# A fast matrix multiplication in a ConvGLU up-projection: the third panel combined in ten of eleven groups, and the order of its weight sums

## The chip, the cores and the metric

The kernel runs on one core of a Trainium2 chip. The core has a matrix engine (TensorE, PE in the profile; its weight loads are PEld), a vector engine (VectorE, DVE), a scalar engine (ScalarE, ACT), a general engine (GpSimd, POOL) and a queue that issues most transfers (SyncE, SP). Each engine works through its own instructions in order and waits on semaphores for the others. Matmuls write into PSUM banks; all else lives in SBUF. The metric is the device time of one execution in microseconds (us); shown is the median of several.

## The reference

One layer of a streaming encoder for two groups of requests: 256 frames of a new stream and 8 x 16 frames of running streams, 384 rows in all. The first half (a convolution branch, an attention branch, gates, an output projection) is not touched by the change. The second half is a ConvGLU feed-forward:

```python
h2 = rmsnorm(x, norm_ffn_g)
up = h2 @ w_up                      # 2048 -> 2 x 5632
g_half = up[..., :D_FF]
u_half = up[..., D_FF:]
ext_f = jnp.concatenate([ffn_buf.astype(g_half.dtype), g_half], axis=1)
gc = causal_dwconv(ext_f, ffn_dw_w, ffn_dw_b)      # 3 taps
x = x + (jax.nn.silu(gc) * u_half) @ w_down
```

All of it is float32.

## The kernel before

**Precision.** Every float32 operand X of a matmul is split into a rounded half `hi` and a remainder `lo = X - hi`, and a product is three matmuls: hi by hi, hi by lo, lo by hi. For a block of weights (2 x 128 rows of 512 columns, 512 KB) the split is a copy on ScalarE (L167, `hi`) and a subtraction on VectorE (L168, `lo`). `ahead` keeps `depth[0]` blocks split in advance: two, and three in the feed-forward part, where a third pair of halves is there. The halves of item i go into the pair that item i-3 has left. The raw blocks come through SyncE (L150) into slots, three at first and seven in the feed-forward part, used in turn.

**The up-projection.** It runs in eleven groups of 512 gate columns and the 512 up columns that belong to them (`up_group`, g = 0 to 10). The 2048 inputs are four panels q of 512. The order of the whole is a list: up 0, up 1, up 2, down (0, 1), up 3, up 4, down (2, 3), and so on to up 9, up 10, down (8, 9, 10). Between two "down" stages there are thus two up groups (three at first).

**Plain and combined panels.** In a plain panel each of the two halves of the rows is an item of its own for the up side (`pu0`, `pu1`) and the gate side (`pg0`, `pg1`): four blocks, four items, 6 products of 3 matmuls each, 24 products in all. In a combined panel the four blocks B11, B12, B21 and B22 are used as in Winograd's form of a fast 2 x 2 multiplication: there are seven items, b22, t3, t1, b11, t2, b21 and t4, of 4, 4, 2, 4, 2, 4 and 2 products, 22 in all. Four of the items are sums of weights, made by VectorE on whole blocks: t3 = B22 + B12 (L209, into one of three sum tiles), t1 = B12 + B11 (L214, in place), t2 = t3 + B11 and t4 = t2 + B21 (L218, in place in the sum tile). Each of the seven is then split like any block. So a combined panel has three splits and four sums more than a plain one, and 6 matmuls less.

Panels 0 and 1 are combined in all groups ("double"); panel 2 (`BOTH`) also in the groups in `TRIPLE`, 3, 5, 7 and 9 ("triple"). A double group has 92 products, 276 matmuls; a triple one 90 products, 270 matmuls. Of panel 2 both kinds of input halves are kept; the combinations of its rows (`xm`) are made by `combined` during the output projection before, a number of ticks (9 matmuls each there) after the panel's output.

**The order within a group** is given by `steps(g)`. The upper pass takes for each combined panel b22, t3, t1, then a plain up item if there is one left to spread, then b11, t2; then come the remaining plain up items; the lower pass starts with `pg0` of the first plain panel and goes on with b21 and t4 of each combined panel. In group 0 no plain item is put into the upper pass. TensorE follows this order as written. VectorE, ScalarE, GpSimd and SyncE are ordered by a scheduler ahead of the run, by what it thinks is ready and by rank: splits and sums are issued with a rank 150 instructions ahead of their place, the evacuations of banks with 250. A sum may so be placed anywhere ahead of the split that needs it.

**Banks and evacuation.** Products add up in five banks `acc` and three `misc`. `q6` (L1225 to L1230) is four operations on VectorE and one on ScalarE, done after the last t2 of the upper pass; it frees the bank of P5, which Q4 takes in the lower pass. `p7` (L1219) and `p1` (L1222) are copies on ScalarE, `q3`, `q2`, `p2`, `q4` (L1234, L1237, L1251, L1254) one operation on VectorE each.

**After a group** come its taps: from the eighth tick of three products on, four times in turn a fill of the extended rows on ScalarE and GpSimd, three taps (L1142 on ScalarE, L1144 twice on VectorE), a SiLU, the product with the up half and its split. They run beside the stage that follows: for groups 0, 1, 3, 5, 7 and 9 that is another up group, for groups 2, 4, 6 and 8 a down stage.

Of the kernel before, what the change touches and what calls it, by code (L numbers as in the profile page):

```python
# [11 lines left out]
ALU = mybir.AluOpType  # L12
# [20 lines left out]
KEYS_FIRST, KEYS_EVERY = 40, 14  # L33
SPLIT_AHEAD, EVAC_AHEAD, FFN_AHEAD = 150, 60, 250
BOTH = 2
TRIPLE = (3, 5, 7, 9)
SPARE = 1


# [9 lines left out]
def hybrid_step(  # L49
# [41 lines left out]
    def f(ap):  # L91
        return ap.bitcast(F32)
# [3 lines left out]
    tt = nc.vector.tensor_tensor  # L96
# [7 lines left out]

    newest = {}

    def queued(d, chain=True):
        e = d.ins.engine
        if chain and e in newest:
            tc.add_manual_dep(d.ins, newest[e], mybir.DependencyInfo(  # L110
                mybir.DependencyClass.NoSync, mybir.DependencyReason.DATA), reason="queue")
        newest[e] = d.ins.name

    def load_x(c, n, sample_queue=None):
# [43 lines left out]
    def split(raw, o, by_row=False):  # L158
        n = splits[0] % depth[0] - 2
        splits[0] += 1  # L160
        if n >= 0:
            hi, lo = pairs_more[n]
        else:
            hi = wp.tile([P, 2, 512], F32R, tag="hi", bufs=2, name="hi")
            lo = wp.tile([P, 2, 512], F32R, tag="lo", bufs=2, name="lo")
        for k in (slice(0, 1), slice(1, 2)) if by_row else (slice(0, 2),):
            nc.scalar.copy(hi[:, k, :o], raw[:, k, :o])  # L167
            tt(lo[:, k, :o], raw[:, k, :o], f(hi[:, k, :o]), op=ALU.subtract)  # L168
        return hi, lo

    plan = []
# [9 lines left out]
    sums, new_sum = {}, []  # L181

    def steps(g):
        mixed = mixed_of(g)
        pu, pg = ([(f"p{side}{h}", q) for q in range(4) if q not in mixed for h in range(2)] for side in "ug")
        n = len(pu) // 2 if g else 0
        top, low = [], pg[:1]
        for i, q in enumerate(mixed):
            top += [(what, q) for what in ("b22", "t3", "t1")] + pu[i:min(i + 1, n)]
            top += [(what, q) for what in ("b11", "t2")]  # L190
            low += [("b21", q), ("t4", q)] + (pg[i + 1:i + 2] if len(mixed) == 2 else [])
        return top + pu[n:] + low + pg[len(mixed) + 1 if len(mixed) == 2 else 1:]

    def planned_mixed(w, c1, c2, g):
        held = {}

        def load(rows):
            return fetch([rows])[0]
# [4 lines left out]
        def single(name, k, c):  # L203
            held[name] = load(rows_of(w, k, c, 512))
            return held[name]

        def both(q):
            sums[q] = new_sum[0](q)
            tt(sums[q], held["b22"][:], single("b12", 4 * q, c2)[:], op=ALU.add)  # L209
            return sums[q]  # L210

        def across(q):
            b = held["b12"][:]
            tt(b, b, single("b11", 4 * q, c1)[:], op=ALU.add)  # L214
            return b

        def grown(q, name):
            tt(sums[q], sums[q], held[name][:], op=ALU.add)  # L218
            return sums[q]

        make = {"b22": lambda q: single("b22", 4 * q + 2, c2), "t3": both, "t1": across,
# [2 lines left out]
        for what, q in steps(g):  # L224
            if what[0] == "p":
                k, c = 4 * q + 2 * int(what[2]), {"u": c2, "g": c1}[what[1]]
# [38 lines left out]
    def after(units, fn):  # L265
        later.append([units, fn])
# [391 lines left out]
    z, e, r, s2, pl = tiny("lz"), tiny("le"), tiny("lr"), tiny("ls"), tiny("lpoly")  # L658
# [98 lines left out]
    def load_v(h):  # L757
# [14 lines left out]
                  k=kv[h // 4][:, :, :, h % 4, :]) for h in range(H)]  # L772
# [100 lines left out]
    for h in range(H):  # L873
        v = heads[h]["q"]
        hi, lo = (natural(aHL[h // 4][:, i, h % 4, :]) for i in range(2))
# [134 lines left out]
    def combined(n, d):  # L1010
# [22 lines left out]
        def plain():  # L1033
            hi, lo = xm[n]
            for j, (t, h) in enumerate(((0, 0), (0, 1), (1, 1), (2, 0), (2, 1))):
                nc.scalar.copy(blocks(hi[:, 5 + j]), of(t, h))
                tt(blocks(lo[:, 5 + j]), of(t, h), blocks(f(hi[:, 5 + j])), op=ALU.subtract)
        later_by = 5 if n == BOTH else 0
        after(5 + later_by, add_up)
        after(6 + later_by, halves)  # L1040
        if n not in xg:
            after(7, plain)

# [306 lines left out]
```

## Time and profile before

| | |
|---|---|
| Median of 3 runs (lowest, highest) | 1977.36 us (1973.34, 1980.31) |
| Profiled execution, its own time | 1976.67 us |
| Its span, first to last instruction | 1975.0 us |
| Mean granted TensorE clock | 0.999 |
| All waits of TensorE after 850 us that the profile names | 8.5 us |
| VectorE: subtractions waiting for the copy on ScalarE, from 913 us on | 226.6 us |
| VectorE: first sums (L209) waiting for a load | 62.3 us |

The profile is that of one execution. In its rows of instructions the first number is the start in us from the span's start, the second the length, then engine, line, operation, and what is written and read; in brackets stands how long the engine had been idle before it, and what ended that. Rows of groups give the count, the busy time, the mean length in ns and, after the bar, the idle time ahead of them. Rows of stretches give for each stretch its length and then the busy time and count of TensorE, its weight loads, VectorE, ScalarE and GpSimd, the granted clock, the share of the transfer engines and GB/s; where only one engine was asked for, only that one stands there. Neighbouring instructions on VectorE overlap a little, so the time from start to start is shorter than an instruction's length.

### The profile page before, as it was taken

To read this page: it belongs to the slowest core of one execution; us is meant where nothing else is said; L and a number is where in the kernel's file an instruction comes from. 1 tells how busy PE (TensorE), PEld (TensorE's weight loads), DVE (VectorE), ACT (ScalarE), POOL (GpSimd) and SP (SyncE) were. 2 spreads that over 40 slices of the span, in tenths; PEclk is the share of its full clock that TensorE was granted. 3 is DMA by queue.
4 is the path that set the end of the run, shared out by engine and by line. 5 is a ranking of instruction groups with operands and counts; after the bars stand their busy time and mean duration, and the time that the engine had idled before them with its cause. 6 is when DMAs were issued, how large, how long until landed. Compare 5 with 4: busy or idle time off the path is not lost.

```text
span 1975.0 us, 24800 instructions
## 1 busy us (share of the span) xinstructions
PE 1956.7 (99%) x9230; PEld 1645.0 (83%) x9230; DVE 1299.3 (66%) x1715; ACT 903.3 (46%) x1310; POOL 270.2 (14%) x525
## 2 busy tenths in 40 slices
PE   9999999999999999999999999999999999999999
PEld 9999878888888888887788887888888888878887
DVE  4478889747465447467688557855885587568853
ACT  5433353555324423445465444554555445444541
POOL 1001121100000002111122200220022012201310
PEclk9999999999999999999999999999999999999999
DMA  6555786665344438666556675567567656656563
GB/s 185 157 170 161 224 240 200 205 183 158 113 129 128 128 128 274 233 209 215 193 178 206 194 181 148 184 207 181 168 185 204 177 169 193 195 160 188 161 234 112
DMA packets 194901, 358.21 MB, mean 181 GB/s; under 512 B 16386, under 2 KB 66557, under 8 KB 194771
## 3 DMA queue, kind: packets, MB, share of 16 engines
q1 hardware_dynamic: 172779, 272.78, 44.6%
q0 software_dynamic: 21680, 83.70, 15.4%
q8 instruction: 72, 1.18, 0.3%
q14 instruction: 50, 0.41, 0.1%
q10 hardware_dynamic: 320, 0.14, 0.0%
HBM read 301.78 MB, written 55.24 MB: 181 GB/s over the span
## 4 chain that ended last, share of the span: by engine, by line
PE 86%; DVE 7%; DMA 4%; issue 1%; ACT 1%; POOL 0%; SPq 0%; DVEq 0%; POOLq 0%; ACTq 0%
PE acc L314 16%; PE acc L315 16%; PE acc L316 16%; PE acc L1174 7%; PE acc L1173 7%; PE acc L1175 7%; DVE lo L168 3%; PE misc L1174 3%; PE misc L1175 3%; PE misc L1173 3%; DVE ut L580 2%; PE acc L311 2%; PE acc L309 2%; PE acc L310 2%; DMA raw<-in_w_up_dram 1%
## 5 line engine op out<-in xcount | busy, mean ns | idle before, releaser
L168 DVE TENSOR_TENSOR lo<-raw,hi 128x1024 fp32r<-128x1024 f32 (+2 forms) x345 | 413.6, 1199 | 378.8 <-ACT hi L167 378.0
L167 ACT CAST hi<-raw 128x1024 fp32r<-128x1024 f32 (+2 forms) x345 | 355.1, 1030 | 619.4 <-PE acc L316 417.9
L314 PE MATMUL acc<-hi,hT 128*128 128x512 f32 (+1 forms) x704 | 270.4, 384 | 0.1
L315 PE MATMUL acc<-lo,hT 128*128 128x512 f32 (+1 forms) x704 | 266.0, 378 | 1.1 <-DVE lo L168 1.1
L316 PE MATMUL acc<-hi,hT 128*128 128x512 f32 (+1 forms) x704 | 265.7, 377 | 0.0
L168 DVE TENSOR_TENSOR lo<-rest,hi 128x1024 fp32r<-128x1024 f32 x136 | 165.6, 1219 | 87.3 <-ACT hi L167 85.9
L167 ACT CAST hi<-rest 128x1024 fp32r<-128x1024 f32 x136 | 142.7, 1050 | 157.8 <-PE acc L1175 71.5
L314 PE MATMUL acc<-hi,act 128*128 128x512 f32 x484 | 188.3, 389 | 0.0
L315 PE MATMUL acc<-lo,act 128*128 128x512 f32 x484 | 188.3, 389 | 0.0
L316 PE MATMUL acc<-hi,act 128*128 128x512 f32 x484 | 188.3, 389 | 0.0
L1173 PE MATMUL acc<-hi,xg 128*128 128x512 f32 x384 | 150.8, 393 | 3.2 <-ACT xg L1065 2.7
L315 PEld LDWEIGHTS acc<-lo,hT 128*128 128x128 f32 x704 | 132.3, 188 | 25.1 <-DVE lo L168 3.9
L580 DVE SCALAR_TENSOR_TENSOR ut<-ext,cw,ut 128x384 f32<-128x384 f32 x240 | 148.9, 620 | 5.5
L314 PEld LDWEIGHTS acc<-hi,hT 128*128 128x128 f32 x704 | 132.2, 188 | 24.2 <-issue 1.8
L316 PEld LDWEIGHTS acc<-hi,hT 128*128 128x128 f32 x704 | 132.1, 188 | 22.6
L1174 PE MATMUL acc<-lo,xg 128*128 128x512 f32 x384 | 150.2, 391 | 0.7 <-DVE lo L168 0.7
L1175 PE MATMUL acc<-hi,xg 128*128 128x512 f32 x384 | 149.9, 390 | 0.0
L1174 PE MATMUL acc<-lo,xm 128*128 128x512 f32 x340 | 132.8, 390 | 3.6 <-DVE lo L168 3.6
L1173 PE MATMUL acc<-hi,xm 128*128 128x512 f32 x340 | 132.4, 389 | 0.6 <-ACT acc L1052 0.6
L334 POOL DMA_DIRECT2D turn<-block x124 | 69.1, 564 | 466.3 <-DVE block L329 450.3
L1175 PE MATMUL acc<-hi,xm 128*128 128x512 f32 x340 | 132.3, 389 | 0.0
L167 ACT CAST hi<-sums 128x1024 fp32r<-128x1024 f32 x78 | 82.0, 1051 | 75.1 <-PE misc L1175 32.6
(358 smaller groups left out, 3678.0 us busy)
## 6 DMA issues: line engine op xcount, KB each, us to landing
rest<-in_w_up_dram SPq DMA_DIRECT2D x97, 512.0 KB
raw<-in_w_in_dram SPq DMA_DIRECT2D x96, 512.0 KB
raw<-in_w_up_dram SPq DMA_DIRECT2D x79, 512.0 KB
raw<-in_w_down_dram SPq DMA_DIRECT2D x49, 512.0 KB
turn<-block POOLq DMA_DIRECT2D x120, 192.0 KB, 4.8
block<-turn POOLq DMA_DIRECT2D x30, 768.0 KB, 5.8
rest<-in_w_down_dram SPq DMA_DIRECT2D x39, 512.0 KB
raw<-in_w_in_dram SPq DMA_DIRECT2D x64, 256.0 KB
```

The costliest lines, as they stand in the source:

```text
L167: nc.scalar.copy(hi[:, k, :o], raw[:, k, :o])
L168: tt(lo[:, k, :o], raw[:, k, :o], f(hi[:, k, :o]), op=ALU.subtract)
L309: mm(o, hi[:, kk, s], ah, start=st, stop=False)
L310: mm(o, hi[:, kk, s], al, start=False, stop=False)
L314: mm(o, ah[:, s], hi[:, kk, :n], start=st, stop=False)
L315: mm(o, ah[:, s], lo[:, kk, :n], start=False, stop=False)
L316: mm(o, al[:, s], hi[:, kk, :n], start=False, stop=sp)
L334: nc.gpsimd.dma_start(d[:, :, i, :].rearrange("j r n -> r j n"), src[32 * i:32 * i + 32, :].rearrange("r (j n) -> r j n", j=4))
L580: stt(o, v, wc, o, op0=ALU.mult, op1=ALU.add)
L1173: mm(o, ah, hi[:, kk, :], start=st, stop=False)
L1174: mm(o, ah, lo[:, kk, :], start=False, stop=False)
L1175: mm(o, al, hi[:, kk, :], start=False, stop=last[b] == (i, n))
```

## The change

Four edits. `TRIPLE` holds all groups from 1 to 10, so panel 2 is combined everywhere but in group 0. A sum of weights is bound on VectorE behind the subtraction of the item before it in the list (an order without a semaphore). In triple groups the lower pass begins with b21 and t4 of panel 0, and the two gate items of panel 3 follow t4 of panel 0 and of panel 2; the order of double groups is as it was. The combinations of panel 2's rows are made five ticks earlier.

```diff
-TRIPLE = (3, 5, 7, 9)
+TRIPLE = (1, 2, 3, 4, 5, 6, 7, 8, 9, 10)
...
+    def behind(d, name):
+        tc.add_manual_dep(d.ins, name, mybir.DependencyInfo(
+            mybir.DependencyClass.NoSync, mybir.DependencyReason.DATA), reason="queue")
+
     def queued(d, chain=True):
         e = d.ins.engine
         if chain and e in newest:
-            tc.add_manual_dep(d.ins, newest[e], mybir.DependencyInfo(
-                mybir.DependencyClass.NoSync, mybir.DependencyReason.DATA), reason="queue")
+            behind(d, newest[e])
         newest[e] = d.ins.name
...
             nc.scalar.copy(hi[:, k, :o], raw[:, k, :o])
-            tt(lo[:, k, :o], raw[:, k, :o], f(hi[:, k, :o]), op=ALU.subtract)
+            newest["lo"] = tt(lo[:, k, :o], raw[:, k, :o], f(hi[:, k, :o]), op=ALU.subtract).ins.name
...
-        top, low = [], pg[:1]
+        top, low = [], []
         for i, q in enumerate(mixed):
             top += [(what, q) for what in ("b22", "t3", "t1")] + pu[i:min(i + 1, n)]
             top += [(what, q) for what in ("b11", "t2")]
-            low += [("b21", q), ("t4", q)] + (pg[i + 1:i + 2] if len(mixed) == 2 else [])
-        return top + pu[n:] + low + pg[len(mixed) + 1 if len(mixed) == 2 else 1:]
+            low += [[("b21", q), ("t4", q)]]
+        if len(mixed) == 2:
+            return top + pu[n:] + pg[:1] + low[0] + pg[1:2] + low[1] + pg[2:]
+        return top + pu[n:] + low[0] + pg[:1] + low[1] + low[2] + pg[1:]
...
+        def add_to(dst, a, b):
+            behind(tt(dst, a, b, op=ALU.add), newest["lo"])
...
-            tt(sums[q], held["b22"][:], single("b12", 4 * q, c2)[:], op=ALU.add)
+            add_to(sums[q], held["b22"][:], single("b12", 4 * q, c2)[:])
...
-            tt(b, b, single("b11", 4 * q, c1)[:], op=ALU.add)
+            add_to(b, b, single("b11", 4 * q, c1)[:])
...
-            tt(sums[q], sums[q], held[name][:], op=ALU.add)
+            add_to(sums[q], sums[q], held[name][:])
...
-        later_by = 5 if n == BOTH else 0
-        after(5 + later_by, add_up)
-        after(6 + later_by, halves)
+        after(5, add_up)
+        after(6, halves)
```

## The prediction

> **What bounds the kernel now.** The page's first part comes first. It shows TensorE busy for the whole span, so time is won or lost by taking matmuls away or by letting TensorE wait.
>
> ```profile
> PE 1956.7 (99%) x9230; PEld 1645.0 (83%) x9230; DVE 1299.3 (66%) x1715; ACT 903.3 (46%) x1310; POOL 270.2 (14%) x525
> ```
>
> The change touches the eleven up-projection groups only, so I next read the order of time on TensorE and took the first matmul of each group (found by counting 276 matmuls for a double group and 270 for a triple one from the first one on).
>
> ```profile
> 981.88 0.39 PE L1173 MATMUL acc<-hi,xm 128*128 128x512 f32 x1
> 1045.63 0.39 PE L1173 MATMUL acc<-hi,xm 128*128 128x512 f32 x1
> 1108.48 0.39 PE L314 MATMUL acc<-hi,act 128*128 128x512 f32 x1
> ...
> 1173.76 0.39 PE L1173 MATMUL acc<-hi,xm 128*128 128x512 f32 x1
> 1237.84 0.39 PE L1173 MATMUL acc<-hi,xm 128*128 128x512 f32 x1
> 1300.40 0.39 PE L314 MATMUL acc<-hi,act 128*128 128x512 f32 x1
> ...
> 1365.68 0.39 PE L1173 MATMUL acc<-hi,xm 128*128 128x512 f32 x1
> 1427.77 0.39 PE L1173 MATMUL acc<-hi,xm 128*128 128x512 f32 x1
> ...
> 1555.61 0.39 PE L1173 MATMUL acc<-hi,xm 128*128 128x512 f32 x1
> 1617.87 0.39 PE L1173 MATMUL acc<-hi,xm 128*128 128x512 f32 x1
> ...
> 1745.74 0.39 PE L1173 MATMUL acc<-hi,xm 128*128 128x512 f32 x1
> 1809.98 0.39 PE L1173 MATMUL acc<-hi,xm 128*128 128x512 f32 x1
> ```
>
> Group 4 (1237.84 to 1300.40) takes 62.56 us for 276 matmuls: 0.2267 us from one to the next, with no gap. That is the price of a matmul; the 0.39 in the rows is its overlapped length. A clean triple group would take 270 x 0.2267 = 61.20 us. Against these two lengths, group 1 (63.75 us) stalls 1.19, group 2 (62.85) 0.29, and the triple groups 3 (64.08), 5 (62.09), 7 (62.26) and 9 (64.24) stall 2.88, 0.89, 1.06 and 3.04: together **9.35 us** of TensorE waiting in groups 1 to 10. Groups 6, 8 and 10 I take to be like group 4.
>
> What is behind the larger of them can be read in the order of time inside group 3:
>
> ```profile
> 1182.84 1.23 DVE L209 TENSOR_TENSOR sums<-raw 128x1024 f32<-128x1024 f32 x1 [3.86 <-DMA raw<-in_w_up_dram]
> 1183.98 1.22 DVE L168 TENSOR_TENSOR lo<-raw,hi 128x1024 fp32r<-128x1024 f32 x1
> 1185.26 0.50 PE L1174 MATMUL misc<-lo,xm 128*128 128x512 f32 x1 [0.23 <-DVE lo L168]
> ...
> 1188.83 1.23 DVE L214 TENSOR_TENSOR raw<-raw 128x1024 f32<-128x1024 f32 x1 [2.49 <-DMA raw<-in_w_up_dram]
> 1189.97 1.22 DVE L168 TENSOR_TENSOR lo<-rest,hi 128x1024 fp32r<-128x1024 f32 x1
> 1191.11 1.22 DVE L168 TENSOR_TENSOR lo<-sums,hi 128x1024 fp32r<-128x1024 f32 x1
> 1191.24 0.50 PE L1174 MATMUL acc<-lo,xm 128*128 128x512 f32 x1 [1.61 <-DVE lo L168]
> ```
>
> A weight sum stands in VectorE's queue ahead of its turn, waits 3.86 and 2.49 us for a load, and the subtraction queued behind it is late for TensorE. Two subtractions in a row start 1.14 us apart (1189.97, 1191.11): that is VectorE's price of one.
>
> **The change part by part.** *Matmuls removed.* A plain panel issues 24 products, a combined one 22, three matmuls each. Six groups (1, 2, 4, 6, 8, 10) become triple: 6 x 6 x 0.2267 = **8.16 us** less.
>
> *Binding, what it removes.* A sum can no longer stand ahead of the preceding subtraction, so the load waits above can't hold one up. With B21 first, Q4 is begun 12 matmuls (2.7 us) later, and its bank is free by then; this row is the present wait for that bank.
>
> ```profile
> L1173 PEld LDWEIGHTS acc<-hi,xg 128*128 128x128 f32 x304 | 57.1, 188 | 13.9 <-DVE block L1230 2.2
> ```
>
> It is 2.2 us over the four triple groups and is part of the 9.35. I count the whole 9.35 as gone and put into one number, below, all that TensorE will wait instead.
>
> *Binding, what it adds.* The sum of item i now follows the subtraction of item i-1, the rounding copy of i on ScalarE needs that sum, and the subtraction of i needs the copy. Nothing of this can run early, although three pairs of halves are there. Group 0 already shows one such chain, because its loads came late:
>
> ```profile
> 919.65 1.22 DVE L218 TENSOR_TENSOR sums<-sums,raw 128x1024 f32<-128x1024 f32 x1
> 920.78 1.22 DVE L214 TENSOR_TENSOR rest<-rest,rest 128x1024 f32<-128x1024 f32 x1
> 920.98 1.05 ACT L167 CAST hi<-sums 128x1024 fp32r<-128x1024 f32 x1 [2.79 <-DVE sums L218]
> 921.92 0.68 DVE L1051 TENSOR_TENSOR y<-acc,y 128x512 f32<-128x512 f32 x1
> 922.52 1.22 DVE L168 TENSOR_TENSOR lo<-sums,hi 128x1024 fp32r<-128x1024 f32 x1
> ```
>
> The sum starts at 919.65, the copy 1.33 later; it ends 1.05 after that, and a free VectorE would begin the subtraction 0.03 on: 2.41 us from sum to subtraction (here 2.87, as two foreign operations filled the hole and overran it). With the subtraction's own 1.14 a bound item takes 3.55. The upper pass of one combined panel has three bound items (T3, T1, T2) and two others (B22, B11): 3 x 3.55 + 2 x 1.14 = 12.93 us, beside 48 matmuls, 10.88 us. The first panel carries an 18-matmul item of the plain panel (4.08 us for 1.14), so 14.07 fit into 14.96. The second and third panel of a triple group now follow each other with nothing between, and the chain is 2.05 us too long for each.
>
> The stock that it can draw on at their start is the full lead of a subtraction:
>
> ```profile
> 1248.92 1.05 ACT L167 CAST hi<-rest 128x1024 fp32r<-128x1024 f32 x1 [3.02 <-PE acc L1175]
> 1250.00 1.23 DVE L168 TENSOR_TENSOR lo<-rest,hi 128x1024 fp32r<-128x1024 f32 x1 [2.77 <-ACT hi L167]
> 1252.80 0.39 PE L1173 MATMUL acc<-hi,xm 128*128 128x512 f32 x1
> ```
>
> The copy waited for the pair, the subtraction is done at 1251.23, TensorE needs it one matmul after 1252.80, at 1253.03: 1.80 us. From the subtraction of B22 in panel two to that of T2 in panel three the chain takes 12.93 + 3 x 3.55 + 1.14 = 24.72; TensorE goes from the one to the other in 10.88 + 42 x 0.2267 = 20.40. So a triple group stalls 24.72 - 20.40 - 1.80 = **2.5 us**, if VectorE takes subtractions strictly in plan order. In the lower pass B21 and T4 take 4.69 against 36/2 = 18 matmuls, 4.08; 1.2 us short for two of them, inside the stock.
>
> The other end is nothing: each bound item leaves VectorE idle for 2.41 - 1.14 = 1.27 us, and the unbound subtractions of B11 and B22 would fit there, which makes the panel 10.65 us. I stay near the row: the rows of group 3 have the subtractions in plan order, and a pair only comes free three items back, too late for most holes. I take 2.0 us for groups 3, 5, 7 and 9, whose VectorE has little else.
>
> *Groups 1, 2, 4, 6, 8 and 10 have the taps of the group before them.*
>
> ```profile
> 1173.80:1239.80 66.00, 64.03 (x280) 52.05 (x279) 49.46 (x48) 31.66 (x34) 3.66 (x6) 1.00 0.57 163
> 1239.80:1300.40 60.60, 60.60 (x270) 50.15 (x268) 47.52 (x56) 32.45 (x42) 16.09 (x29) 1.00 0.63 193
> ...
> 1264.05 0.71 ACT L1142 ACTIVATE rest<-extf,col,fw 128x384 f32<-128x384 f32 x1 [1.83 <-POOL extf L1130]
> 1264.67 1.03 ACT L167 CAST hi<-rest 128x1024 fp32r<-128x1024 f32 x1
> ...
> L1144 DVE SCALAR_TENSOR_TENSOR rest<-extf,fw,rest 128x384 f32<-128x384 f32 x80 | 47.4, 614 | 8.1 <-ACT rest L1142 7.7
> ```
>
> The stretch table (DVE is the third busy column) gives group 4 47.5 us on VectorE. Three more splits and four more sums add 7 x 1.14 = 8.0: 55.5 of 61.2 us. That is room in the sum, not in the second and third panel, which is where the taps fall (they start eight ticks after the group before, some 18 us in). A tap of 0.61 us fits a hole, but ScalarE's queue is in order, and its tap operation waits 1.83 us for POOL ahead of a copy: now hidden by the stock, later not. Price from nothing to one such wait per panel, 3.7; I take 1.1, so 3.1 us a group. The extra 3 x 1.05 us of copies on ScalarE (32.5 of 60.6 busy) hide beside this.
>
> *Rest.* Each group still loads 16 blocks. A load waits for its slot's last reader; the sum that now waits at 1182.84 would be due near 1200, so loads have some 17 us to spare: nothing. Group 0 is bound too, and both its panels follow each other, up to 2.5; but it waits for the last input panel anyway (the rows below), which hides it: nothing, from -1.6 (the clock loss below, if the wait shrinks) to +2.5. Panel two's combinations move five ticks forward, within an output projection in which VectorE is busy 43 of 73 us:
>
> ```profile
> 840.00:913.00 73.00, 73.00 (x324) 60.40 (x323) 43.08 (x58) 33.47 (x50) 7.98 (x13) 1.00 0.64 208
> ```
>
> Nothing; if they delay that panel, the group-0 wait grows by up to 2.
>
> **Sum.** With s the mean new stall of a group, the time is 1976.67 - 8.16 - 9.35 + 10 s. s = (4 x 2.0 + 6 x 3.1)/10 = 2.66 gives 1985.8 for the profiled execution (its span is 1975.0); the median of the runs, 1977.36, lies 0.7 higher, so I predict **1986.5 us**, 0.46% slower. About 0.3% (6 us) is what a measurement can tell from no change. Break-even is s = 1.75; faster by 0.3% below s = 1.15, slower by 0.3% above 2.35.
>
> **Rivals.** *The holes are used (not slower).* Place: panels two and three; B11's and B22's subtractions stand in the 1.27 us holes, the panel needs 10.65, s is 0 to 1, say 0.6 for the group starts: 1965.9. For it: splits rank ahead of all other work on VectorE, and group 4 loses nothing today although VectorE works 24.6 of these 26 us in its middle:
>
> ```profile
> 1262.00:1288.00 26.00, 24.60 (x35) 1.00 0.46 137
> ```
>
> Against: pairs come free late. It decides below s = 1.15; chance 0.20. *Half of it:* s near 1.7, 1977: 0.27. *The taps break the chain everywhere:* 2.5 and 4.5 us, s = 3.7, 1997: 0.10; what speaks for it is the 1.83 us wait above, against it that splits rank first. *The clock.* After an idle time TensorE runs at half rate:
>
> ```profile
> 947.56 0.80 PE L1173 MATMUL acc<-hi,xg 128*128 128x512 f32 x1 [2.74 <-ACT xg L1065]
> 950.72 0.46 PE L1174 MATMUL acc<-lo,xg 128*128 128x512 f32 x1
> 951.25 0.40 PE L1173 MATMUL acc<-hi,xg 128*128 128x512 f32 x1
> ```
>
> From 947.56 to 950.72 lie seven matmuls (six are left out), 0.45 us each where 0.2267 is the price: 1.6 us lost. Were each group's stalls to do that, 10 x 1.6 more: 2002; chance 0.03, as the 1.61 us wait at 1191.24 was followed by full rate. [...] Forecast proper (s from 2.35 to 3.5, 1982.7 to 1994): 0.40.
>
> **Chances and range.** Slower 0.40 + 0.10 + 0.03 = 0.53, same 0.27, faster 0.20. The range 1968 to 2000 leaves out about one tenth at each end: the full use of the holes, and taps or clock at their worst.
>
> **What would show it.** Matmuls: 36 fewer, groups 4, 6, 8 and 10 of 270. Chain: TensorE waits for L168 at T2 of panel two and T3, T1, T2 of panel three, each under 1 us; ScalarE's copies of sums waiting for L209, L214 and L218; VectorE's load waits before L209 gone. Taps: larger stalls in even groups than in odd ones. It is wrong if the second and third panel show no waits for L168, or if the subtractions of B11 stand before those of T1.

## The result, and the profile after

The changed kernel takes **2001.5 us** (median of 4 runs, 2000.17 to 2002.46) against 1976.69 beside it: ratio 1.0122, interval 1.0108 to 1.0135. It is slower, as forecast, but by 1.22% and not by 0.46%, and it lies just above the range. The profiled execution took 2000.17 us, its span is 1998.5.

Lines have moved: the copies are now L170, the subtractions L171, all sums L203 (one helper), the matmuls of the up groups L1180 to L1182, those of the down stages L322 to L324, the transposes L337. First the page's engine totals and one of its groups of instructions, of the changed kernel:

```profile
PE 1959.1 (98%) x9194; PEld 1636.9 (82%) x9194; DVE 1348.7 (67%) x1757; ACT 917.7 (46%) x1328; POOL 269.8 (14%) x525
...
L170 ACT CAST hi<-sums 128x1024 fp32r<-128x1024 f32 x96 | 100.9, 1051 | 185.2 <-DVE sums L203 161.3
```

The 36 matmuls are gone (9230 to 9194). The second row is the binding: ScalarE is idle for 185.2 us ahead of copies of sums, 161.3 of it for the sum itself (before: 78 such copies, 75.1 us idle, mostly for TensorE to free a pair). The bill is that TensorE waits for subtractions in combined panels.

The three largest waits of TensorE from 850 us on, changed kernel (engine, line and what it waited for; us in total, times, longest):

```profile
PE acc L1181 <- DVE lo L171: 17.8, 27, 1.5
PE misc L1181 <- DVE lo L171: 7.5, 10, 0.9
PE acc L322 <- ACT act L1160: 3.8, 1, 3.8
```

VectorE's table of the same stretch has no wait for a load any more; before it had 74.3 us of them, 62.3 at L209 alone:

```profile
DVE sums L209 <- DMA rest<-in_w_up_dram: 34.9, 10, 5.5
DVE sums L209 <- DMA raw<-in_w_up_dram: 27.4, 7, 6.4
```

So the binding did what it says, and a worse wait took the place of the one removed. The stretch table of the changed kernel shows where (length, then busy time of PE, PEld, DVE, ACT and POOL with their counts, the clock, DMA): groups 1, 2, 3, 4, 10 and the last down stage with what follows.

```profile
977.27:1045.10 67.83, 64.13 (x272) 51.52 (x270) 58.62 (x67) 38.09 (x48) 14.04 (x28) 0.97 0.51 152
1045.10:1110.74 65.64, 62.72 (x271) 50.30 (x270) 58.97 (x67) 36.52 (x47) 15.59 (x25) 1.00 0.54 170
...
1176.03:1239.80 63.77, 62.25 (x272) 50.37 (x270) 48.15 (x46) 29.31 (x32) 3.10 (x5) 1.00 0.53 150
1239.80:1305.66 65.86, 62.91 (x271) 50.30 (x270) 58.52 (x66) 36.37 (x46) 14.16 (x25) 1.00 0.50 167
...
1824.45:1890.28 65.83, 62.86 (x272) 50.30 (x270) 58.75 (x66) 36.64 (x47) 14.70 (x26) 1.00 0.45 148
1890.28:1998.50 108.22, 99.99 (x433) 81.82 (x431) 47.12 (x56) 32.52 (x40) 13.78 (x30) 0.98 0.54 180
```

A clean triple group is 61.20 us. By their lengths less 61.20, the stalls are 6.6 (group 1), 4.4 (group 2), 2.6 (3) and 4.7 (4); from there it repeats: 5, 7 and 9 stall 2.59, 2.59 and 2.54; 6, 8 and 10 stall 4.59, 4.59 and 4.62. Together **39.8 us** in groups 1 to 10, against 9.35 before. The last down stage, clean before, stalls 5.7; group 0 stalls 3.33 instead of 6.14; the up stage began 1.8 earlier in this execution. Balance of the spans: -8.16 - 9.35 + 39.8 + 5.7 - 2.8 - 1.8 = +23.4; the spans differ by 23.5 (1975.0 to 1998.5). (Kernels that are the same up to that place began it up to 1.5 us apart, so the 1.8 may be nothing but scatter.)

Now group 3, which has no taps. Order of time on VectorE and ScalarE, changed kernel (start, length, then in brackets the idle time before and what ended it):

```profile
1189.37 1.22 DVE L203 TENSOR_TENSOR sums<-rest,rest 128x1024 f32<-128x1024 f32 x1
1190.70 1.05 ACT L170 CAST hi<-sums 128x1024 fp32r<-128x1024 f32 x1 [2.50 <-DVE sums L203]
1191.78 1.22 DVE L171 TENSOR_TENSOR lo<-sums,hi 128x1024 fp32r<-128x1024 f32 x1 [1.19 <-ACT hi L170]
1192.93 1.22 DVE L203 TENSOR_TENSOR rest<-rest,rest 128x1024 f32<-128x1024 f32 x1
```

This is the forecast chain to the hundredth: 2.41 us from sum to subtraction (1189.37 to 1191.78), 3.56 from one bound sum to the next. TensorE's gaps that follow from it:

```profile
1201.58 0.50 PE L1181 MATMUL misc<-lo,xm 128*128 128x512 f32 x1 [0.58 <-DVE lo L171]
1209.31 0.50 PE L1181 MATMUL acc<-lo,xm 128*128 128x512 f32 x1 [0.64 <-DVE lo L171]
1222.17 0.50 PE L1181 MATMUL acc<-lo,xm 128*128 128x512 f32 x1 [0.30 <-DVE lo L171]
```

They stand at T2 of panel two, T1 of panel three and, in the lower pass, T4 of panel one (panels counted from one). A gap of 0.58 costs about 0.28 more, since the matmul behind it shows 0.50 us where its pitch is 0.2267; by first matmuls the three items stall 0.88, 0.92 and 0.61.

Group 4, which has the taps of group 3 in it:

```profile
1265.77 1.22 DVE L203 TENSOR_TENSOR sums<-raw,rest 128x1024 f32<-128x1024 f32 x1
1267.21 1.31 ACT L1149 ACTIVATE rest<-extf,col,fw 128x384 f32<-128x384 f32 x2 [1.97 <-POOL extf L1137]
1268.42 1.04 ACT L170 CAST hi<-sums 128x1024 fp32r<-128x1024 f32 x1
1269.62 1.22 DVE L171 TENSOR_TENSOR lo<-sums,hi 128x1024 fp32r<-128x1024 f32 x1
1270.89 0.50 PE L1181 MATMUL acc<-lo,xm 128*128 128x512 f32 x1 [0.88 <-DVE lo L171]
```

The sum's result is there 1.33 us after its start, as above, at 1267.10. But ScalarE holds a tap operation that waits for POOL, with a second one behind it, and the copy starts at 1268.42: 1.3 us late, and with no lead left TensorE pays 0.88 and the 0.28. In group 1 the same pair stands ahead of T2's copy in panel two, with the copy of the next B22 behind it, so that T2's copy is 2.25 us late (it starts at 1002.44; its sum began at 998.86), and there the clock goes down as well:

```profile
1000.29 1.31 ACT L1149 ACTIVATE rest<-extf,col,fw 128x384 f32<-128x384 f32 x2 [1.96 <-POOL extf L1137]
...
1003.54 0.50 PE L1180 MATMUL misc<-hi,xm 128*128 128x512 f32 x1 [1.52 <-ACT hi L170]
1004.99 0.50 PE L1181 MATMUL misc<-lo,xm 128*128 128x512 f32 x1 [0.95 <-DVE lo L171]
...
1005.90 0.63 PE L1181 MATMUL misc<-lo,xm 128*128 128x512 f32 x1
1006.33 0.63 PE L1182 MATMUL misc<-hi,xm 128*128 128x512 f32 x1
```

Matmuls now stand 0.43 apart, until 1008.89: seven such steps and two half ones, some 1.6 us lost.

The last down stage is another story, of the operations that nobody binds. VectorE, then TensorE, changed kernel:

```profile
1877.20 0.70 DVE L337 STREAM_TRANSPOSE block<-block 128x512 f32<-128x512 f32 x1
...
1882.73 0.70 DVE L337 STREAM_TRANSPOSE block<-block 128x512 f32<-128x512 f32 x1
...
1889.33 0.70 DVE L337 STREAM_TRANSPOSE block<-block 128x512 f32<-128x512 f32 x1
...
1900.87 1.89 DVE L337 STREAM_TRANSPOSE block<-block 128x512 f32<-128x512 f32 x3
...
1926.92 0.55 PE L322 MATMUL acc<-hi,act 128*128 128x512 f32 x1 [3.85 <-ACT act L1160]
```

The three transposes of group 10's up rows are spread over 12 us among the chain and the taps of group 9. The gate rows' transposes wait for them (both use one work tile), and the activation of group 10 comes 3.85 us late for the last down stage. Before, the same transposes stood at 1853.21 and 1855.44, and the gate rows' at 1872.73.

### The profile page after: what moved, and what is told of

The parts are those of the page before. It is cut to its first block, busy times and chain, and to the rows that moved or that the text cites. A ratio compares the mean times of both kernels' runs of the same rounds, so it can differ in the third digit from the quotient of the medians.

```text
span 1998.5 us, 24776 instructions
## 1 busy us (share of the span) xinstructions
PE 1959.1 (98%) x9194; PEld 1636.9 (82%) x9194; DVE 1348.7 (67%) x1757; ACT 917.7 (46%) x1328; POOL 269.8 (14%) x525
## 4 chain that ended last, share of the span: by engine, by line
PE 86%; DVE 8%; ACT 2%; issue 2%; POOL 1%; ACTq 0%; DVEq 0%; POOLq 0%
PE acc L322 17%; PE acc L323 17%; PE acc L324 17%; PE acc L1181 6%; PE acc L1182 6%; PE acc L1180 6%; DVE lo L171 5%; PE misc L1181 3%; PE misc L1182 2%; PE misc L1180 2%; PE acc L319 2%; PE acc L317 2%; PE acc L318 2%; ACT hi L170 2%; DVE sums L203 1%
## 5 line engine op out<-in xcount | busy, mean ns | idle before, releaser
L171 DVE TENSOR_TENSOR lo<-raw,hi 128x1024 fp32r<-128x1024 f32 (+2 forms) x345 | 413.0, 1199 | 383.0 <-ACT hi L170 382.5
L170 ACT CAST hi<-raw 128x1024 fp32r<-128x1024 f32 (+2 forms) x345 | 354.4, 1029 | 590.5 <-PE acc L324 406.5
L322 PE MATMUL acc<-hi,hT 128*128 128x512 f32 (+1 forms) x704 | 270.4, 384 | 0.1
L324 PE MATMUL acc<-hi,hT 128*128 128x512 f32 (+1 forms) x704 | 265.6, 377 | 0.0
L171 DVE TENSOR_TENSOR lo<-rest,hi 128x1024 fp32r<-128x1024 f32 x136 | 165.0, 1222 | 109.7 <-ACT hi L170 109.2
L170 ACT CAST hi<-rest 128x1024 fp32r<-128x1024 f32 x136 | 141.7, 1048 | 124.9 <-PE acc L324 35.9
L322 PE MATMUL acc<-hi,act 128*128 128x512 f32 x484 | 188.9, 390 | 3.8 <-ACT act L1160 3.8
L324 PE MATMUL acc<-hi,act 128*128 128x512 f32 x484 | 189.0, 390 | 0.0
L170 ACT CAST hi<-sums 128x1024 fp32r<-128x1024 f32 x96 | 100.9, 1051 | 185.2 <-DVE sums L203 161.3
L1181 PE MATMUL acc<-lo,xm 128*128 128x512 f32 x388 | 155.3, 400 | 17.9 <-DVE lo L171 17.8
L171 DVE TENSOR_TENSOR lo<-sums,hi 128x1024 fp32r<-128x1024 f32 x96 | 116.9, 1217 | 53.9 <-ACT hi L170 53.8
L1180 PE MATMUL acc<-hi,xm 128*128 128x512 f32 x388 | 152.0, 392 | 0.2
L322 PEld LDWEIGHTS acc<-hi,hT 128*128 128x128 f32 x704 | 132.2, 188 | 24.1 <-issue 1.8
L1182 PE MATMUL acc<-hi,xm 128*128 128x512 f32 x388 | 151.6, 391 | 0.0
L324 PEld LDWEIGHTS acc<-hi,hT 128*128 128x128 f32 x704 | 132.1, 188 | 22.8
L1181 PE MATMUL acc<-lo,xg 128*128 128x512 f32 x300 | 116.8, 389 | 0.0
L1180 PE MATMUL acc<-hi,xg 128*128 128x512 f32 x300 | 116.7, 389 | 0.0
```

Source lines behind the costliest of these rows:

```text
L171: newest["lo"] = tt(lo[:, k, :o], raw[:, k, :o], f(hi[:, k, :o]), op=ALU.subtract).ins.name
L322: mm(o, ah[:, s], hi[:, kk, :n], start=st, stop=False)
L324: mm(o, al[:, s], hi[:, kk, :n], start=False, stop=sp)
L1180: mm(o, ah, hi[:, kk, :], start=st, stop=False)
L1181: mm(o, ah, lo[:, kk, :], start=False, stop=False)
L1182: mm(o, al, hi[:, kk, :], start=False, stop=last[b] == (i, n))
```

## The experiments

Theory A: the tight order "subtraction, sum, copy, subtraction" takes the sums' lead away, and taps in ScalarE's and VectorE's queues then cost their full length. Theory B: it is the triple groups themselves (more sums, loads, the banks' order), and the binding matters little. "Stall" of a group is its length from first to first matmul less 0.2267 us a matmul, read from the one profiled execution of each kernel.

| kernel | us | ratio to before, interval | odd triple groups stall | even triple groups stall | last down stage |
|---|---|---|---|---|---|
| changed | 2001.5 | 1.0122, 1.0108 to 1.0135 | 2.57 | 4.6 | 5.7 |
| unbound | 1984.5 | 1.0038, 1.0023 to 1.0053 | 0.7 to 3.9 | 1.6 to 3.3 | 0 |
| triple groups only | 1987.8 | 1.0049, 1.003 to 1.0069 | 0.8 to 3.0 | 2.7 to 3.6 | 0 |
| bound only | 1983.8 | 1.0032, 1.0019 to 1.0045 | 3.38 | (double) 0.95 | 0 |
| bound one earlier | 1968.3 | 0.9953, 0.9938 to 0.9968 | 0 | 1.1 | 5.4 |
| bound two earlier | 1988.0 | 1.0056, 1.0039 to 1.0073 | 0.25 | 4.26 | 6.9 |
| taps due later | 1996.3 | 1.0096, 1.008 to 1.0111 | 2.55 | 4.7 | 0 |
| taps bound later | 1993.3 | 1.0085, 1.007 to 1.01 | 2.5 | 5.0 | 0 |
| plain item later | 1997.7 | 1.0104, 1.009 to 1.0118 | 2.48 | 4.37 | 6.9 |
| turn ahead | 2010.7 | 1.0171, 1.0158 to 1.0185 | 4.3 | 5.95 | 0 |
| one earlier, turn ahead | 1971.9 | 0.9974, 0.9963 to 0.9984 | 1.0 | 1.75 | 0 |
| one earlier, turn ahead in group 10 | 1966.7 | 0.9948, 0.9936 to 0.9961 | 0 | 1.06 | 0 |
| the same, taps bound later | 1963.1 | 0.9933, 0.992 to 0.9945 | 0 | 0.70 | 0 |

Odd triple groups are 3, 5, 7 and 9, even ones 4, 6 and 8, which follow them with nothing between. Group 10 stalls as the even ones do, but for 5.9 with triple groups only, 3.7 with the taps bound later, and 2.83 and 2.48 in the last two rows.

### Unbound

```
-            behind(tt(dst, a, b, op=ALU.add), newest["lo"])
+            tt(dst, a, b, op=ALU.add)
```

> The changed kernel with its weight sums unbound again; the ten triple groups, B21 first and the earlier combinations stay. Theory A, the chain (a bound sum makes subtraction, sum, copy and next subtraction follow one another, 12.93 us a panel beside 10.88 of matmuls): the stalls of 2.6 us (groups 3, 5, 7, 9) and 4.6 us (4, 6, 8, 10) go, at most 1 us a group is left for load waits, and the wait of the last down stage goes too: about 1970 us, 1965 to 1976. Theory B, the load (the third panel brings VectorE to its limit in groups that hold taps, however the sums stand): groups 4, 6, 8 and 10 still stall by some 4 us and the last down stage still waits: 1988 to 1998 us.

1984.5 us, between the two ranges. It keeps the 36 matmuls less and B21 first, and is 17 us under the changed kernel by their medians, so most of that kernel's loss is the binding. But it isn't faster than before either: the old load waits are back, in VectorE's waits of this kernel (the first two of six rows, which sum to 87.6 us; before, 74.3):

```profile
DVE sums L203 <- DMA rest<-in_w_up_dram: 33.8, 19, 4.2
DVE sums L203 <- DMA raw<-in_w_up_dram: 32.5, 14, 4.9
```

More sums that stand ahead of their turn cost more of what they cost before. Something had to be done about them; the tight binding was more than that.

### Bound only

The kernel before with the binding, and nothing else:

```
-TRIPLE = (1, 2, 3, 4, 5, 6, 7, 8, 9, 10)
+TRIPLE = (3, 5, 7, 9)
...
+        return top + pu[n:] + pg[:1] + low[0] + low[1] + low[2] + pg[1:]
...
+        later_by = 5 if n == BOTH else 0
```

> The kernel before with the binding alone: triple groups 3, 5, 7 and 9, the old order of the lower pass, the old time of the combinations. Theory A: the four triple groups stall 2.6 us each plus 0.5 at the start of the lower pass, about 12 us where they had 7.8; double groups have a plain item in both panels and stall under 0.5; group 0 wins about 3: 1975 to 1981 us, no clear change. Theory B (binding only takes the load waits away): 1966 to 1971 us.

1983.8 us: slower, if just above theory A's range. The binding alone costs. Odd groups stall 3.38, of which this row, in TensorE's waits of this kernel, is the wait for Q4's bank that B21 first takes away (4.5 us over four groups):

```profile
PE acc L1181 <- DVE block L1238: 4.5, 4, 1.1
```

3.38 less 1.1 is 2.3, near the changed kernel's 2.57 in the same groups. The double groups 4, 6, 8 and 10 stall about 0.95 each, not under 0.5 as theory A had it; before, they stalled nothing. Group 0 stalls 3.30 here, with panel two's combinations where they were before: the binding alone is enough to shorten its stall from 6.14, without the earlier combinations.

### Triple groups only

Unbound, with the old order of the lower pass:

```
-        return top + pu[n:] + low[0] + pg[:1] + low[1] + low[2] + pg[1:]
+        return top + pu[n:] + pg[:1] + low[0] + low[1] + low[2] + pg[1:]
```

> Ten triple groups and the earlier combinations alone: sums unbound, lower pass beginning with the plain gate item. Theory A: as the unbound kernel, plus the wait for Q4's bank of 0.5 us in each of ten groups: 5 us above it, some 1975 us. Theory B: 1993 to 2003 us. If it equals the unbound kernel, B21 first brings nothing.

1987.8 us, between the two theories, and 3.3 above the unbound kernel beside it. The intervals of the two overlap, but their waits differ: for the operation that frees Q4's bank (L1237) TensorE waits 5.0 us here and 0.3 us there, which is about what B21 first is worth. Neither part of the change pays by itself without the sums' place being right.

### Bound one earlier

The test that tells most: the same matmuls, sums and order of panels, but each sum may stand one subtraction ahead.

```
+            newest["older"] = newest.get("lo")
             newest["lo"] = tt(lo[:, k, :o], raw[:, k, :o], f(hi[:, k, :o]), op=ALU.subtract).ins.name
...
-            behind(tt(dst, a, b, op=ALU.add), newest["lo"])
+            behind(tt(dst, a, b, op=ALU.add), newest["older"])
```

> The changed kernel with each sum bound not behind the subtraction of the item before, but behind that of the item before that one, so a sum may stand in the 1.27 us hole while the copy of the item before runs. Theory A: the panel takes its VectorE work only (8 x 1.14 = 9.1 us beside 10.88), stalls fall under 1 us a group in odd groups and to 1 or 2 in groups with taps: 1966 to 1978 us. Theory B: the same VectorE work, so as the changed kernel, 1996 to 2003 us.

1968.3 us, faster than both kernels. The stretch of group 3, and VectorE and ScalarE within it, of this kernel (subtractions are L172, sums L204):

```profile
1169.77:1230.97 61.20, 61.20 (x272) 50.70 (x270) 49.93 (x48) 30.16 (x32) 3.10 (x5) 1.00 0.58 162
```

```profile
1187.20 1.22 DVE L204 TENSOR_TENSOR sums<-sums,rest 128x1024 f32<-128x1024 f32 x1
1188.77 1.23 DVE L172 TENSOR_TENSOR lo<-rest,hi 128x1024 fp32r<-128x1024 f32 x1 [0.36 <-ACT hi L170]
1190.41 1.05 ACT L170 CAST hi<-sums 128x1024 fp32r<-128x1024 f32 x1 [1.67 <-PE acc L1183]
1191.50 1.23 DVE L172 TENSOR_TENSOR lo<-sums,hi 128x1024 fp32r<-128x1024 f32 x1 [1.50 <-ACT hi L170]
```

61.20 us is the clean length, with no less work on VectorE (49.93 us; 48.15 in the changed kernel's group 3). The sum now ends while the item before is subtracted, and the copy waits for TensorE to free a pair, not for the sum. Waits for loads are 0.4 us in all. So the odd groups' 2.57 us were the chain; theory B, by which the time would have stayed at 1996 to 2003, falls.

### Bound two earlier

```
+            newest["oldest"] = newest.get("older")
+            newest["older"] = newest.get("lo")
...
-            behind(tt(dst, a, b, op=ALU.add), newest["lo"])
+            behind(tt(dst, a, b, op=ALU.add), newest["oldest"])
```

> The changed kernel with each sum bound behind the subtraction of three items before instead of the one before (two items earlier than in the change, one earlier than in the run that took 1968.34). The series is then: directly behind the preceding subtraction 2001.5, one earlier 1968.34, two earlier, and no binding 1984.5. If a sum that stands too early waits for its loads and holds up the subtractions behind it, as without a binding (87.6 us of waits of sums for loads), this lies between one earlier and none: 1969 to 1982, with sums waiting for loads by 5 to 60 us. If the unbound kernel lost by another thing than the early place (which subtraction stands ahead, say), this is no slower than one earlier: 1964 to 1969, with hardly a wait for loads.

1988.0 us, outside both expectations, and sums wait for loads by 0.6 us in all. Odd groups stay near nothing (0.25); the even ones, with taps, stall 4.26: in group 4 1.2 at T3 of panel three and, in the lower pass, 1.85 at T4 of panel one and 0.86 at the gate item behind it. At T4 TensorE waits for the bank that Q4 takes. ScalarE has the tap operation ahead of a copy again; `q6`, which frees the bank, has its ScalarE operation behind both (at 1277.35), and its last operation on VectorE (L1239) ends at 1281.41:

```profile
1275.38 0.71 ACT L1151 ACTIVATE rest<-extf,col,fw 128x384 f32<-128x384 f32 x1 [2.08 <-POOL extf L1139]
1276.00 1.03 ACT L170 CAST hi<-sums 128x1024 fp32r<-128x1024 f32 x1
...
1281.46 0.50 PE L1182 MATMUL acc<-hi,xm 128*128 128x512 f32 x1 [1.58 <-DVE block L1239]
```

So the trace puts the even groups' stall down to the taps and to the bank; no run took the two apart. Of the last down stage's 6.9 us, a wait of 3.85 and then some 3 us at half rate are in the trace. Why the sums' earlier place brings all this back is open. What holds is that the best place is one between the change's and none at all, and that it was found by measuring, not by theory.

### Taps due later, and taps bound later

First their due time alone, for groups 0, 1, 3, 5, 7 and 9:

```
-            lag, pace = (7, 1) if g == 10 else (8, 2)
+            lag, pace = (7, 1) if g == 10 else (19 if g in (0, 1, 3, 5, 7, 9) else 8, 2)
```

> The changed kernel with the taps of groups 0, 1, 3, 5, 7 and 9 begun at tick 19 instead of 8 of the group that follows, so that they fall in its lower pass and not in panels two and three. If the taps' operations in ScalarE's and VectorE's queues are what makes groups 4, 6, 8 and 10 stall 4.6 us where groups 3, 5, 7 and 9 stall 2.6, those four fall to 2.6 to 3.2, and groups 1 and 2 by as much: 8 to 12 us less than the changed kernel, 1989 to 1994, unless the last down stage waits longer. If the price is that of the chain alone, or of the group before ending without a down stage, they stay at 4 to 5 and the time at 2000.

1996.3 us, between the two times expected; the even groups are unchanged (4.6 to 4.75), as the second expectation had it, because the first taps did not move: in this kernel, too, they stand ahead of the copy in panel three.

```profile
1268.60 1.31 ACT L1149 ACTIVATE rest<-extf,col,fw 128x384 f32<-128x384 f32 x2 [1.97 <-POOL extf L1137]
1269.81 1.04 ACT L170 CAST hi<-sums 128x1024 fp32r<-128x1024 f32 x1
```

Here a later place in the program was no later place in the queue. (The 5 us won are the last down stage.) So the copy that opens each tap item was bound as well, with the same due times:

```
-            nc.scalar.copy(hi[:, k, :o], raw[:, k, :o])
+            newest["hi"] = nc.scalar.copy(hi[:, k, :o], raw[:, k, :o]).ins.name
...
-                nc.scalar.copy(e[:, :, 2:18]...)
+                behind(nc.scalar.copy(e[:, :, 2:18]...), newest["hi"])
```

> The changed kernel, with the tap work that belongs to groups 0, 1, 3, 5, 7 and 9 due 11 ticks later (behind the third panel of the following group's upper pass), and the ScalarE copy that opens each tap item bound in its queue behind the newest hi copy at its place in the program, so that, unlike in the run with the due time alone, it can't be placed ahead of it. Theory A: the even groups' stall of 4.6 us against the odd groups' 2.56 comes from tap operations that stand ahead of copies and sums of panels 2 and 3 in ScalarE's and VectorE's queues; then even groups fall to 2.6 to 3.2, group 1 from 6.6 to about 3, group 2 from 4.4 to about 3, together 10 to 14 us: 1987 to 1992. Rival B: the even groups' longer stall comes from something else that only they have (the down stage ahead is behind odd groups, not even ones; their up rows' turn), then they stay at 4.2 to 5 and the time is 1998 to 2004. Rival C: the taps cost as much among the lower pass's sums, where each panel has one bound pair; then the stall moves from T3 and T1 to T4 and the time is 1996 to 2004.

1993.3 us, between theory A's range and rival C's, and a split answer. The upper pass of group 4 now stalls 2.7 us (T1 of panel two 0.95; T1, B11 and T2 of panel three 0.83, 0.16 and 0.76), about what odd groups stall; in the changed kernel nearly all of its 4.65 fell there, 1.29 of them at the T3 behind the tap operation. But the lower pass, clean before, now stalls 2.2, at B21 and T4 of panel three, where the moved taps stand on VectorE:

```profile
1295.79 1.14 DVE L1151 SCALAR_TENSOR_TENSOR rest<-extf,fw,rest 128x384 f32<-128x384 f32 x2
1296.85 1.21 DVE L171 TENSOR_TENSOR lo<-rest,hi 128x1024 fp32r<-128x1024 f32 x1
...
1299.25 0.50 PE L1181 MATMUL acc<-lo,xg 128*128 128x512 f32 x1 [1.45 <-DVE lo L171]
```

So the 2.0 us between even and odd groups are the taps, as theory A has it, and in both places tried they cost it where they meet the tight chain, as rival C has it. The even groups' total of 5.0 alone would fit rival B, but the places of the stall moved with the taps. The 8 us won are group 1, which stalls 2.55 instead of 6.6 (1.6 of that is the half rate, which did not come), and the clean last down stage, less 1.7 us lost in group 2.

### Plain item later

In triple groups the plain panel's first upper item was moved from panel one into panel two, behind its T1, to give the chain its 18 matmuls near the stall:

```
+            between = pu[i:min(i + 1, n)] if len(mixed) == 2 else pu[:1] if i == 1 else []
-            top += [(what, q) for what in ("b22", "t3", "t1")] + pu[i:min(i + 1, n)]
+            top += [(what, q) for what in ("b22", "t3", "t1")] + between
```

> The changed kernel with the one plain up item of a triple group moved from panel one to panel two, nothing else. The chain's arithmetic: panel one, alone now, is 2.05 us too long, which the lead at a group's start (4 to 6 us after a down stage, 3 after a group) carries; panel two fits with the 18 extra matmuls; panel three is 11.79 - 9.52 - 1.80 = 0.5 us too long. Groups 3, 5, 7 and 9 stall 0.5 to 1.1 us instead of 2.6, the others about 2 less: 1983 to 1990 us. If the stalls came from what the queues hold rather than from the chain, moving one plain item would move them and not lessen them: 1998 to 2004.

1997.7 us; odd groups 2.48, not 0.5 to 1.1. The expectation failed: T1 of panel two, which now has no long item ahead of it, stalls 0.94, T1 of panel three 0.92, T4 0.59. The likely reason is that a long item gives back at most one item's lead, because a copy can't start before its pair comes free three items back: around the long item three copies of group 3 wait for TensorE, 1.58, 1.76 and 2.23 us. A lead would then not be a stock to be saved up; no run tried that by itself.

### The turn of the up rows ahead

All groups' turns of up rows ranked like the evacuations, first on the changed kernel, then on the one bound one earlier:

```
-            ups[g] = turned_rows("u", 0)
+            with tc.high_priority(offset=FFN_AHEAD):
+                ups[g] = turned_rows("u", 0)
```

> The changed kernel with the turn of the up rows (three transposes on VectorE and the transfers behind them) ranked like the evacuations instead of last. If the last down stage waits for the last group's activations because those transposes found no room (5.5 and 6.6 us apart in the changed kernel, 2.2 before), its stall of 5.7 us goes to 0 and the time falls by about that, to 1995 to 1998; the transposes may cost the chain up to 1 us a group, then no change. If the activations are late for the taps' own sake, the stall stays.

> Each sum bound behind the subtraction one item earlier, and the turn of the up rows ranked with the evacuations: the two that go together if each does what is thought of it. The last down stage loses its 5.4 us of stall, the groups stay at 0 (3, 5, 7, 9) and about 1 (the others): 1961 to 1965 us, 0.6 to 0.9% faster than the kernel before.

2010.7 and 1971.9 us, both slower than expected. The last down stage's stall is gone in both, which shows that the transposes' place caused it. But three transposes ahead of subtractions in every group cost more than that: odd groups go from 2.57 to 4.3, and from 0 to 1.0 in the looser kernel. Only group 10 needs them early, so then in group 10 alone:

```
+            if g == 10:
+                with tc.high_priority(offset=FFN_AHEAD):
+                    ups[g] = turned_rows("u", 0)
+            else:
+                ups[g] = turned_rows("u", 0)
```

> The kernel with each sum bound one subtraction earlier (1968.34), with the turn of the up rows (its three transposes) ranked like the evacuations in group 10 alone. Theory: the wait of 5.4 us in the last down stage comes from transposes that stand late behind the chain in group 10 only; ranked ahead there, the wait goes and groups 1 to 9 stay as they were (0 in odd ones, 1.05 in even ones): 1962 to 1965. Rival: in group 10 the transposes ahead hold up the chain and the banks as they did in every group when all groups had them so (1.0 to 1.7 us more a group), or the last down stage's wait comes from the gate rows; then 1965 to 1968.5.

1966.7 us: the last down stage is clean, but group 10's own stall goes from 1.1 to 2.83, most of it (2.1) at the gate item of the plain panel. The gain of 5.4 is partly given back, as the rival said, and the intervals of this and of the kernel without it overlap. With the taps bound later beside it:

> Both together: each sum bound one subtraction earlier, taps of groups 0, 1, 3, 5, 7 and 9 later and bound behind the newest hi copy, the turn of the up rows ranked ahead in group 10 alone. If the 1.05 us left in each even group (and 0.9 in groups 1 and 2) with the looser binding are the taps too, some 4 to 6 us go against the run beside it with the taps where they were: 1957 to 1961. If they are not, or if the later taps meet the lower pass's sums, 1961 to 1968.

**1963.1 us**, 0.67% faster than before (0.55 to 0.80), and the best of these kernels. Groups 1, 2, 4, 6 and 8 stall 0.7 instead of 0.9 to 1.1; between this and the kernel without it lie 3.7 us by the medians, 2.2 by the spans of the profiled executions (1963.5 and 1961.3), and 1.9 by the stalls of groups 1 to 10 (7.8 and 5.9), short of the 4 to 6 expected. Its group 4 in the stretch table, 0.7 over the clean length:

```profile
1230.06:1291.97 61.91, 61.51 (x271) 50.60 (x270) 54.05 (x59) 34.25 (x41) 15.08 (x27) 1.00 0.57 185
```

What is left there is group 0 with 5.0 us and group 10 with 2.5. In group 0, which is double and kept the old order of its lower pass, 2.5 of it are one wait for Q4's bank (at 954.23, shown at the end) and 1.6 the half rate behind that wait.

## Why the prediction was right or wrong

**Right: what bounds it, and the sign.** The 36 matmuls went, at 0.2267 us; the load waits went; B21 first removed the wait for Q4's bank. TensorE's new waits are for L171, stalls are larger in even groups than in odd ones, and copies of sums wait for sums, as the last part of the prediction asked.

**Right: the chain.** 2.41 us from sum to subtraction and 2.5 us a triple group were worked out; 2.41 and 2.57 are measured, and loosening the order by one item takes all of the 2.57 away. Taking 2.0 of it, because holes would be used, was an error of 0.57 in four groups, 2.3 us. One hole was used in group 3 (the subtraction of a B22 at 1199.17 stands ahead of T2's at 1200.31). Of the four places named, T2 of panel two and T1 of panel three wait there, T3 and T2 of panel three do not; and the lower pass, which the prediction had "inside the stock", lost 0.6 at T4.

**Wrong: the taps' term.** Of the sum's terms this one was furthest off: 1.1 us a group was taken from a range of 0 to 3.7; measured are 2.0 in groups 4, 6, 8 and 10, 1.9 in group 2, and 4.1 in group 1 (1.6 of it the half rate), against the odd groups' 2.57. The mechanism was named right (the tap operation that waits for POOL ahead of a copy: 1.97 us at 1267.21); the size was read from a trace in which it was covered. With the forecast's 2.0 and 3.1 a group the sum of stalls was 26.6; it is 39.8, 2.3 of the difference from the odd groups and 10.9 from these six: 5.9 the taps, 3.4 the chain's 0.57 once more, 1.6 the half rate. The rival "the taps break the chain everywhere", with 2.5 and 4.5 us and a chance of 0.10, is what happened, nearly to the number in its stalls. Two smaller slips stand beside it: the 47.5 us of VectorE are those of a stretch that begins 2 us behind group 4's first matmul (the whole group has 49.5, so 57.5 of 61.2 were to be expected, and 58.5 came); and the bounds 1982.7 and 1994 lack the 0.7 us that the forecast and the rivals have in them.

**Missing: the last down stage.** 5.7 us that no step of the prediction mentions: a wait of 3.85 and 1.7 at half rate behind it. It asked what a change costs the matmuls of its own groups, and not what else VectorE does among them (the transposes of group 10's up rows) and who at the far end waits for that. With the rival's 1997 us, these 5.7 less group 0's 2.8 and the earlier start's 1.8 would have been 1998.

**Group 0** was put at nothing, from -1.6 to +2.5; it gained 2.8, just outside, and the kernel with nothing but the binding gains as much. Of these, 1.6 are the half rate that no longer came, as the prediction's -1.6 had it.

**The clock.** The rival in which every group's stalls halve the rate did not come. The rate halved twice: for some eight matmuls in group 1, after waits of 1.52 and 0.95 us, and for nine behind the 3.85 us wait of the last down stage, 1.6 to 1.7 us each time; both are inside the stalls above. The wait of 1.52 us in group 1 is longer than any stall that was forecast, each under 1 us. The two waits in group 1 sum to 2.47 us, and the wait of the last down stage is one of 3.85; what more the traces show of the rate stands in the last section.

**Open:** why binding two items earlier brings the taps' and the bank's waits back in the even groups, and why the wait for Q4's bank in group 0 appears only with the binding one item earlier; neither was taken apart. That group 0 stalls 4.9 to 5.1 us in three of those kernels and 3.4 in the one with every group's turn ahead is the half rate alone: the wait is 2.38 us in all four.

## What to carry to other kernels

Binding an order to stop one operation from standing too early also stops it from being early at all: here directly behind the preceding subtraction cost 1.2%, one item looser gained 0.5% with the same work, and two items looser or no binding cost 0.4 to 0.6%; so look for the loosest binding that still removes the wait, and measure its neighbours. When a change takes the lead out of a chain, price every other operation in that chain's queues at its full length and wait, not at what it cost while the lead covered it. And follow the low-ranked work in those queues (here three transposes) to its own user, which may be a stage further on.

## What the runs showed of the hardware that was not expected

TensorE's rate halved after two short waits close together, 1.52 and 0.95 us with a single matmul of 0.50 us between them (it starts at 1003.54, and the next, after its wait of 0.95, at 1004.99): the matmuls behind them stand 0.43 us apart where 0.2267 is the price. Single waits of 0.88 us (1270.89) or 1.51 us (931.08 in group 0, the first row below) left it at full rate. And one wait of 2.38 us, in group 0, was followed by half rate in one kernel (the second row, of the last kernel of the table) and by full rate in another (the third, of one earlier with the turn ahead):

```profile
931.08 0.50 PE L1181 MATMUL acc<-lo,xm 128*128 128x512 f32 x1 [1.51 <-DVE lo L171]
...
954.23 0.50 PE L1181 MATMUL acc<-hi,xg 128*128 128x512 f32 x1 [2.38 <-DVE block L1238]
...
954.26 0.50 PE L1181 MATMUL acc<-hi,xg 128*128 128x512 f32 x1 [2.38 <-DVE block L1238]
```

The clock that the traces record differs between the two. Behind the wait nine matmuls fill 3.42 us at a clock of 0.50 in the first of these kernels, and seventeen fill 3.41 us at 1.00 in the other (length, then busy time and matmuls of TensorE, the clock, DMA):

```profile
954.75:958.17 3.42, 3.42 (x9) 0.50 0.10 20
...
955.85:959.26 3.41, 3.41 (x17) 1.00 0.31 67
```

While matmuls run, the recorded clock is 0.50 in two stretches of the changed kernel's execution, from 1005.64 to 1009.05 and from 1927.24 to 1930.65, and in one of the kernel before, from 947.45 to 950.86, 3.41 us each. In these executions, then, single waits of 0.88, 1.51 and 1.61 us (the last at 1191.24 in the kernel before) were followed by full rate, single waits of 2.74 us (947.56 there) and 3.85 us and the two that sum to 2.47 us by half rate, and the wait of 2.38 us by the one or the other. So the length of a single wait alone does not settle it; what does is not shown, and no run was made for it.
